# Two-layer hybrid encoder trunk: a new written order of the mixers' steps, with the output projection cut into half-steps

## The chip, the cores and the metric

The kernel runs on one core of a Trainium2 chip, in one launch. The metric is the device time of an execution in microseconds. The kernel before took 1021.98 us, the median of three runs (1021.69 to 1022.37).

Engine names are those of the profile: PE is the matrix engine (PEld its weight loads), DVE the vector engine, ACT the scalar engine, POOL the general one, and SP the queue that issues the weight transfers.

## The reference, cut to what matters

The input is 256 tokens of width 1024, in float32. Each of two layers does a half-step SwiGLU, a mixer, and a second half-step SwiGLU:

```python
for l in range(DEPTH):
    h_res = h_res + 0.5 * swiglu(rmsnorm(h_res, ffn1_norm[l]), ...)
    z = rmsnorm(h_res, mix_norm[l]) @ w_in[l]
    zq, zk, zv, zp, hq, hi, hff, hfb, hg = jnp.split(z, split_idx, axis=-1)
    y_att = dilated_attention(zq, zk, zv, q_norm[l], k_norm[l], biases)
    y_pool = pool_mixer(zp, pool_w[l], pool_scale[l])
    y_rec = hgrn2_bidirectional(hq, hi, hff, hfb, hg, ...)
    h_res = h_res + jnp.concatenate([y_att, y_pool, y_rec], axis=-1) @ w_out[l]
    h_res = h_res + 0.5 * swiglu(rmsnorm(h_res, ffn2_norm[l]), ...)
```

The attention has 8 heads of 64 with normalised queries and keys, a relative bias and a softmax. The pooling mixer has four window sizes. The recurrence (HGRN2) has 4 heads of 64 and runs in both directions. The concatenated 1024 columns go through one output projection of 1024 x 1024.

## The kernel before

Every large product is made of three float32r products: each operand is split into a high part (an ACT copy) and a low part (a DVE subtraction). The weights come as 512 KB "halves". For each half SP issues a transfer into one of four stage buffers, ACT makes `whi` (L149) and DVE `wlo` (L150). There are five buffers for split halves, and `ahead(i)` asks for the split of half i + 4 when half i is about to be used.

The text changed is in `mixer`. A step list `ORDER[l]`, one for each layer, writes out the order in which the mixer's steps are issued. PE and SP run exactly in the order of the program (`manual_schedule` for these two). DVE, ACT and POOL run fixed queues too, but their order is chosen when the kernel is built, by a planner: it takes what it believes to be ready, the earliest written first, and the steps `ga`, `gb`, `uv` and `up` are ranked ahead of their place. The planner also hands out the buffers of a pool. So a step's place in the list fixes PE's order, and influences that of DVE and ACT.

The steps, by their names in the list:

- `c:0` to `c:19` are the input projection's halves in the order hq, q, k, zh (pooling inputs and recurrence values), hg, v; q, k, zh and v take four quarter-steps each of 12 products of 512 columns, hq and hg two steps of 24 products of 256 columns. When the last one of a name is issued, its evacuation is issued: `qk_evac` (with squares and sums), `tok_evac` for zh and v, `hg_evac` (a chain of four ACT and three DVE operations).
- `ns`, `nq`, `nk` scale and turn the queries and keys into columns: four transposes, then a high part by ACT (L669, L675) and a low part by DVE (L670, L676).
- `mm:m`, `up:m`, `put:m` are the levels of the recurrence: 32 or 64 small products, the update of U and W by DVE (L523), and the storing of the result by DVE (L569) or ACT (L574, L579, L583). `join`, `rec`, `rn1`, `rn2` finish it: `rec` multiplies into `ops`, `rn1` squares and splits, `rn2` sums by two products (`hss`) and normalises.
- `sc:n` scores two heads: 12 products into two PSUM banks, then the softmax of each head. DVE adds the bias and takes the extreme (L701), ACT exponentiates (L704), DVE takes the reciprocal and scales (L706, L708).
- `tr:h` turns a head's probabilities (four transposes, L715) and ACT copies them out (L717). `pv:n` multiplies two heads by the values (L727); an odd one splits the result (L257, L258).
- `band`, `pool` make the pooling mixer: 16 products (L741) and a copy (L745), then 4 products (L751), two ACT and two DVE operations (L756, L757) on one bank.
- `o:name` is one quarter of the output projection's contraction, by `down`: two halves, `dh` 0 and 1, of 12 products of 512 columns each, into four tiles `wo`.

PSUM has eight banks, in two pools of four. Pool `pg` (tag "g") holds the projection's accumulators, the turns of q and k, scores, `pbs`, `hss`, `pps`, `pv` and, before, `ops`. Pool `py` (tag "y") holds the levels' results, the turned probabilities `tp`, and at the end the four `wo` tiles.

Of the kernel before, what the change touches and what calls it, by code (L numbers as in the profile page):

```python
# [8 lines left out]
F32 = mybir.dt.float32  # L9
# [7 lines left out]
P = 128  # L17
D = 1024
T = 256
# [24 lines left out]
OUT_NAMES = ("pool", "rec", "a0", "a1")  # L44
# [2 lines left out]

ORDER = (
    (
# [4 lines left out]
    ),  # L54
    (
# [4 lines left out]
    ),  # L60
)
LOOK = 4
# [8 lines left out]
class Trunk:  # L71
# [161 lines left out]
                self.mm3t(accs[tt], self.xh[:, k, s], self.xl[:, k, s], wh[:, kk, :], wl[:, kk, :],  # L233
                          start=(k == 0), stop=(k == KC - 1))

    def down(self, i, ys, ah, al, first, last, mid=None, post=None):

        for dh in range(2):
            self.ahead(i + dh)
            wh, wl = self.half(i + dh, 2)  # L240
            for tt in range(2):
                s = slice(tt * P, tt * P + P)
                for f in range(2):
                    self.mm3t(ys[2 * dh + tt], ah[:, f, s], al[:, f, s], wh[:, f, :], wl[:, f, :],
                              start=(first and f == 0), stop=(last and f == 1))
                if post is not None:
                    post(dh, tt)
            if dh == 0 and mid is not None:
                mid()
# [202 lines left out]
    def mixer(self, l):  # L452
        nc = self.nc
        mx, pg, py = self.mx, self.pg, self.py
        i0 = self.cur
        o0 = i0 + IN_HALVES
        V = {}
# [4 lines left out]
        def bank(name):  # L462
            return pg.tile([P, 2, T], F32, tag="g", name=name)
# [124 lines left out]
                nc.vector.tensor_copy(V["Ad"][p, :, p], V["A"][p])  # L588

        def rec_mm():  # L590
            ops = V["ops"] = bank("ops")
            vh = V["vh"]
            for hp in range(2):
                for e in range(2):
                    h = 2 * hp + e
                    for tb in range(2):
                        for n, sb in enumerate((tb, 1 - tb)):
                            A = V["Ad"][:, 2 * h + tb, :] if sb == tb else V["Ao"][:, 4 * sb + h, :]
                            nc.tensor.matmul(ops[e * 64:e * 64 + 64, hp, tb * P:tb * P + P],
                                             lhsT=vh[:, sb, h * 64:h * 64 + 64], rhs=A,  # L600
                                             start=(hp == 0 and tb == 0 and n == 0),
                                             stop=(hp == 1 and tb == 1 and n == 1), skip_group_check=True)
# [106 lines left out]

        def att_tr(h):  # L710
            pt = V["P", h]
            tp = py.tile([P, 2, T], F32, tag="y", name="tp")
            for kt in range(2):
                for qt in range(2):
                    nc.tensor.transpose(tp[:, kt, qt * P:qt * P + P], pt[:, qt, kt * P:kt * P + P], self.ident)  # L715
            pT = V["PT", h] = self.t2("PT")
            nc.scalar.activation(pT, tp, AF.Copy)  # L717
# [43 lines left out]
        ga, gb = bank("ga"), bank("gb")  # L761
# [23 lines left out]

        ys = []

        def out(nm):
            n = OUT_NAMES.index(nm)
            if n == 0:  # L790
                ys.extend(py.tile([P, 512], F32, tag="y", name="wo") for _ in range(4))
            src = V["yatt", int(nm[1])] if nm[0] == "a" else V["y" + nm]
            last = n == len(OUT_NAMES) - 1
            if last:
                self.new_xt()
            post = lambda dh, tt: self.add(ys[2 * dh + tt], 1.0, dh, tt, self.to_stage(3 * l + 2))
            self.down(o0 + 2 * n, ys, *src, first=n == 0, last=last, post=post if last else None)

        do = {
            "c": take, "ga": gates_a, "gb": gates_b, "uv": lev_init, "up": lev_up, "mm": lev_mm,  # L800
            "put": lev_put, "join": lev_join, "band": pool_band, "pool": pool_out, "ns": qk_scale, "nq": lambda j: qk_turn("q", j),
            "nk": lambda j: qk_turn("k", j), "sc": att_scores, "tr": att_tr, "pv": att_pv, "rec": rec_mm,
            "rn1": rec_squares, "rn2": rec_norm, "o": out,
        }
        for step in ORDER[l].split():
            nm, _, arg = step.partition(":")
# [163 lines left out]
```

## Time and profile before

| | before |
|---|---|
| median of three runs | 1021.98 us |
| the profiled execution, whole | 1022.51 us |
| its span, first to last instruction | 1020.7 us |
| PE busy | 1002.3 us (98%) |
| DVE busy | 606.7 us (59%) |
| ACT busy | 538.7 us (53%) |
| first mixer, first projection product to first product of the next SwiGLU | 199.95 to 327.46 us |
| second mixer, the same | 703.89 to 830.92 us |

The span is what the profiler saw of the program; the execution's own time has 1.8 us more around it. Times below are in us from the span's start. In a timeline row, a duration is from an instruction's start to the modelled end of its result, so that neighbouring matrix products overlap: their cost is the distance from start to start. "[0.60 <-DVE st L701]" at the end of a row says that the engine sat idle so long just before it, and what ended that. A row with "x4" merges four alike.

### The profile page before, as it was taken

What the parts mean: (1) busy time and instruction counts of PE and PEld (TensorE: products, weight loads), DVE (VectorE), ACT (ScalarE), POOL (GpSimd) and SP (SyncE); (2) the same over time, 40 slices, a digit from 0 to 9 for tenths busy, and PEclk for the clock granted to TensorE, in tenths of its full rate; (3) what the DMA queues carried; (4) which work ended last, traced back from release to release, by engine and by line L of the source; (5) the groups of instructions that cost most, each with busy time, mean ns of one, the idle gap of its engine ahead of it and who ended that gap; (6) DMA issues with size and microseconds to landing.
All of it is one profiled execution on the core that took longest, in us unless ns stands there. A gap on an engine that the chain in (4) does not pass through costs nothing.

```text
span 1020.7 us, 14464 instructions
## 1 busy us (share of the span) xinstructions
PE 1002.3 (98%) x5722; PEld 828.2 (81%) x5722; DVE 606.7 (59%) x811; ACT 538.7 (53%) x774; POOL 3.3 (0%) x8
## 2 busy tenths in 40 slices
PE   8999999999999999999999999999999999999998
PEld 7888788897877888888878888888877778888886
DVE  5555555689955655555565454556998465545453
ACT  7444444675765544444474444446857554444441
POOL 0000100000000000000000000000000000000000
PEclk9999999999999999999999999999999999999999
DMA  7675876544334556555655656554542345556551
GB/s 257 223 258 187 278 257 187 181 148 151 103 107 155 173 186 194 185 194 185 186 165 186 186 188 185 192 188 135 192 142 88 121 155 190 186 188 187 186 187 60
DMA packets 50276, 181.16 MB, mean 177 GB/s; under 512 B 5752, under 2 KB 6008, under 8 KB 49952
## 3 DMA queue, kind: packets, MB, share of 16 engines
q1 hardware_dynamic: 48528, 174.09, 53.4%
q0 software_dynamic: 720, 4.21, 1.2%
q10 hardware_dynamic: 960, 1.94, 0.5%
q8 instruction: 45, 0.74, 0.3%
q14 instruction: 23, 0.19, 0.1%
HBM read 179.15 MB, written 3.16 MB: 179 GB/s over the span
## 4 chain that ended last, share of the span: by engine, by line
PE 84%; DVE 8%; ACT 4%; issue 2%; DMA 1%; SPq 0%; DVEq 0%
PE gu L168 16%; PE gu L170 15%; PE gu L169 15%; PE ya L170 8%; PE ya L168 8%; PE ya L169 8%; DVE wlo L150 2%; ACT whi L149 2%; PE hp L352 2%; PE wo L168 1%; PE wo L170 1%; PE wo L169 1%; DVE P L701 1%; PE xps L294 1%; PE pv L727 1%
## 5 line engine op out<-in xcount | busy, mean ns | idle before, releaser
L150 DVE TENSOR_TENSOR wlo<-stage,whi 128x1024 fp32r<-128x1024 f32 (+1 forms) x329 | 401.4, 1222 | 350.1 <-ACT whi L149 349.3
L149 ACT ACTIVATE whi<-stage 128x1024 fp32r<-128x1024 f32 (+1 forms) x329 | 347.1, 1056 | 369.2 <-PE gu L170 200.1
L168 PE MATMUL gu<-whi,xh 128*128 128x512 f32 x704 | 275.4, 391 | 3.7 <-DVE xl L273 2.2
L170 PE MATMUL gu<-whi,xl 128*128 128x512 f32 x704 | 274.2, 390 | 0.0
L169 PE MATMUL gu<-wlo,xh 128*128 128x512 f32 x704 | 274.0, 389 | 0.0
L168 PEld LDWEIGHTS gu<-whi,xh 128*128 128x128 f32 x704 | 132.2, 188 | 33.1 <-DVE xl L273 2.9
L170 PEld LDWEIGHTS gu<-whi,xl 128*128 128x128 f32 x704 | 132.1, 188 | 28.3 <-DVE xl L273 0.9
L169 PEld LDWEIGHTS gu<-wlo,xh 128*128 128x128 f32 x704 | 132.2, 188 | 27.0
L168 PE MATMUL ya<-whi,hi 128*128 128x512 f32 x352 | 141.5, 402 | 0.0
L170 PE MATMUL ya<-whi,lo 128*128 128x512 f32 x352 | 137.7, 391 | 0.0
L169 PE MATMUL ya<-wlo,hi 128*128 128x512 f32 x352 | 137.3, 390 | 0.0
L170 PEld LDWEIGHTS ya<-whi,lo 128*128 128x128 f32 x352 | 66.0, 188 | 14.4
L169 PEld LDWEIGHTS ya<-wlo,hi 128*128 128x128 f32 x352 | 66.3, 188 | 12.6
L168 PEld LDWEIGHTS ya<-whi,hi 128*128 128x128 f32 x352 | 66.2, 188 | 12.3
L345 ACT ACTIVATE g<-gu,rc 128x256 f32<-128x256 f32 x88 | 41.4, 475 | 47.4 <-PE gu L170 47.4
L346 DVE SCALAR_TENSOR_TENSOR h<-gu,rc,g 128x256 f32<-128x256 f32 x88 | 42.0, 481 | 23.9 <-ACT g L345 23.9
L258 DVE TENSOR_TENSOR lo<-hp,hi 128x512 fp32r<-128x512 f32 x44 | 30.1, 684 | 2.8 <-ACT hi L257 2.8
L257 ACT ACTIVATE hi<-hp 128x512 fp32r<-128x512 f32 x44 | 25.5, 580 | 2.7 <-PE hp L352 2.7
L352 PEld LDWEIGHTS hp<-cst,h 128*128 128x128 f32 x176 | 21.8, 139 | 5.7
L352 PE MATMUL hp<-cst,h 128*128 128x128 f32 x176 | 26.3, 271 | 0.0
L272 ACT ACTIVATE xh<-xps,prm 128x256 fp32r<-128x256 f32 x48 | 20.5, 471 | 5.8 <-DVE xl L273 3.4
L273 DVE SCALAR_TENSOR_TENSOR xl<-xps,prm,xh 128x256 fp32r<-128x256 f32 x48 | 21.3, 478 | 2.4 <-ACT xh L272 2.2
(223 smaller groups left out, 997.5 us busy)
## 6 DMA issues: line engine op xcount, KB each, us to landing
stage<-w_all SPq DMA_DIRECT2D x327, 512.0 KB, 3.5
skew<-drow POOLq DMA_DIRECT2D x1, 2048.0 KB, 10.3
bias<-skew POOLq DMA_DIRECT2D x2, 1024.0 KB, 11.6
x<-x SPq DMA_DIRECT2D x4, 256.0 KB, 5.1
band<-band ACTq DMA_DIRECT2D x1, 1024.0 KB, 7.7
y_t<-x SPq DMA_DIRECT2D x4, 256.0 KB, 2.2
stage<-w_all SPq DMA_DIRECT2D x2, 256.0 KB, 5.5
mskf<-msk ACTq DMA_DIRECT2D x1, 320.0 KB, 5.7
```

The source lines that it names most:

```text
L149: nc.scalar.activation(hi[:, s], st[:, s], AF.Copy)
L150: nc.vector.tensor_tensor(lo[:, s], st[:, s], hi[:, s].bitcast(F32), op=ALU.subtract)
L168: nc.tensor.matmul(out, lhsT=ah, rhs=wh, start=start, stop=False, skip_group_check=True)
L169: nc.tensor.matmul(out, lhsT=ah, rhs=wl, start=False, stop=False, skip_group_check=True)
L170: nc.tensor.matmul(out, lhsT=al, rhs=wh, start=False, stop=stop, skip_group_check=True)
L257: self.nc.scalar.activation(hi, src, AF.Copy)
L258: self.nc.vector.tensor_tensor(lo, src, hi.bitcast(F32), op=ALU.subtract)
L272: nc.scalar.activation(self.xh[:, k, :], src, AF.Copy, scale=g)
L273: nc.vector.scalar_tensor_tensor(self.xl[:, k, :], src, g, self.xh[:, k, :].bitcast(F32), op0=ALU.mult, op1=ALU.subtract)
L345: silu = nc.scalar.activation(g2[:, tt, :], gu[tt][:, 0:256], AF.Silu, scale=r)
L346: nc.vector.scalar_tensor_tensor(h[:, tt, :], gu[tt][:, 256:512], r, g2[:, tt, :], op0=ALU.mult, op1=ALU.mult)
L352: nc.tensor.transpose(hp[:, f, tt * P:tt * P + P], h[:, tt, f * P:f * P + P], self.ident)
```

## The change

Three things change. (1) The two step lists are rewritten. The score steps move later: in the first layer from after c:12, c:13, c:14 and c:15 to after c:13, c:15, c:17 and into the output projection; in the second from after c:13 (two of them), c:14 and c:15 to after c:14, c:15, c:17 and into the output projection. `nq:0 nq:1` follow c:8 in both, and `band` moves from after c:16 to after c:14. In the first layer `nk:0 nk:1` stand together after c:12, the levels from 16 on come one step of c later, and `rec` moves from after c:16 to after c:17. The turns `tr` come mostly in pairs, and the last two, with `sc:3`, `pv:2` and `pv:3`, stand between half-steps of the output projection. (2) `o:name` becomes two steps `o:name/0` and `o:name/1`, by a new argument `dhs` of `down`. (3) `ops` moves from the pool `pg` to `py`, and a turn issued when the `wo` tiles exist takes its bank from `pg`. The instructions and their operands are otherwise the same, in number and shape.

```diff
 ORDER = (
     (
-        "c:0 ga c:1 gb c:2 uv c:3 c:4 mm:0 c:5 put:0 mm:1 up:2 ns:q c:6 put:1 c:7 mm:2 up:4 nq:0 c:8 put:2 nq:1 c:9 mm:4 up:8 ns:k put:4 "
-        "c:10 c:11 mm:8 up:16 put:8 nk:0 c:12 nk:1 mm:16 up:32 put:16 sc:0 c:13 mm:32 up:64 put:32 sc:1 "
-        "c:14 mm:64 up:128 put:64 sc:2 tr:0 c:15 mm:128 put:128 join tr:1 sc:3 c:16 tr:2 band rec rn1 c:17 rn2 tr:3 tr:4 pool c:18 tr:5 tr:6 "
-        "c:19 tr:7 o:pool pv:0 pv:1 o:rec pv:2 pv:3 o:a0 o:a1 "
+        "c:0 ga c:1 gb c:2 uv c:3 c:4 mm:0 c:5 put:0 mm:1 up:2 ns:q c:6 put:1 c:7 mm:2 up:4 c:8 put:2 nq:0 nq:1 c:9 mm:4 up:8 ns:k put:4 "
+        "c:10 c:11 mm:8 up:16 put:8 c:12 nk:0 nk:1 c:13 sc:0 mm:16 up:32 put:16 c:14 mm:32 up:64 put:32 band "
+        "c:15 sc:1 tr:0 tr:1 mm:64 up:128 put:64 c:16 mm:128 put:128 join c:17 rec rn1 sc:2 tr:2 tr:3 c:18 rn2 pool tr:4 tr:5 "
+        "c:19 o:pool/0 pv:0 pv:1 sc:3 o:pool/1 o:rec/0 tr:6 tr:7 o:rec/1 pv:2 pv:3 o:a0/0 o:a0/1 o:a1/0 o:a1/1 "
     ),
     (
-        "c:0 ga c:1 gb c:2 uv c:3 c:4 c:5 mm:0 ns:q put:0 c:6 mm:1 up:2 put:1 c:7 nq:0 c:8 mm:2 up:4 nq:1 put:2 c:9 ns:k mm:4 up:8 put:4 "
-        "c:10 c:11 mm:8 up:16 put:8 c:12 nk:0 nk:1 c:13 sc:0 mm:16 up:32 put:16 sc:1 c:14 mm:32 up:64 put:32 "
-        "sc:2 tr:0 c:15 mm:64 up:128 put:64 tr:1 sc:3 c:16 tr:2 band mm:128 put:128 join c:17 tr:3 tr:4 rec rn1 pool c:18 rn2 tr:5 tr:6 "
-        "c:19 tr:7 o:pool pv:0 pv:1 o:rec pv:2 pv:3 o:a0 o:a1 "
+        "c:0 ga c:1 gb c:2 uv c:3 c:4 c:5 mm:0 ns:q put:0 c:6 mm:1 up:2 put:1 c:7 c:8 nq:0 nq:1 mm:2 up:4 put:2 c:9 ns:k mm:4 up:8 put:4 "
+        "c:10 c:11 mm:8 up:16 put:8 c:12 nk:0 nk:1 c:13 mm:16 up:32 put:16 c:14 mm:32 up:64 put:32 sc:0 band "
+        "c:15 mm:64 up:128 put:64 sc:1 c:16 mm:128 put:128 join tr:0 tr:1 c:17 rec rn1 sc:2 tr:2 c:18 rn2 pool tr:3 tr:4 "
+        "c:19 tr:5 o:pool/0 pv:0 pv:1 sc:3 o:pool/1 o:rec/0 tr:6 tr:7 o:rec/1 pv:2 pv:3 o:a0/0 o:a0/1 o:a1/0 o:a1/1 "
     ),
 )
...
-    def down(self, i, ys, ah, al, first, last, mid=None, post=None):
-
-        for dh in range(2):
+    def down(self, i, ys, ah, al, first, last, mid=None, post=None, dhs=(0, 1)):
+
+        for dh in dhs:
...
         def rec_mm():
-            ops = V["ops"] = bank("ops")
+            ops = V["ops"] = py.tile([P, 2, T], F32, tag="y", name="ops")
...
         def att_tr(h):
             pt = V["P", h]
-            tp = py.tile([P, 2, T], F32, tag="y", name="tp")
+            tp = bank("tp") if ys else py.tile([P, 2, T], F32, tag="y", name="tp")
...
-        def out(nm):
-            n = OUT_NAMES.index(nm)
-            if n == 0:
+        def out(part):
+            nm, dh = part.split("/")
+            n, dh = OUT_NAMES.index(nm), int(dh)
+            if n == 0 and dh == 0:
                 ys.extend(py.tile([P, 512], F32, tag="y", name="wo") for _ in range(4))
             src = V["yatt", int(nm[1])] if nm[0] == "a" else V["y" + nm]
             last = n == len(OUT_NAMES) - 1
-            if last:
+            if last and dh == 0:
                 self.new_xt()
             post = lambda dh, tt: self.add(ys[2 * dh + tt], 1.0, dh, tt, self.to_stage(3 * l + 2))
-            self.down(o0 + 2 * n, ys, *src, first=n == 0, last=last, post=post if last else None)
+            self.down(o0 + 2 * n, ys, *src, first=n == 0, last=last, post=post if last else None, dhs=(dh,))
```

## Rows read from the trace of the kernel before

**Rows 1.** The profile's page, part 1: busy time, share of the span, instructions.

```profile
PE 1002.3 (98%) x5722; PEld 828.2 (81%) x5722; DVE 606.7 (59%) x811; ACT 538.7 (53%) x774; POOL 3.3 (0%) x8
```

**Rows 2.** Waits of PE, first mixer (199 to 330): total us, times, longest.

```profile
PE sc L692 <- DVE Lk L670: 1.2, 1, 1.2
...
PE tp L666 <- DVE zk L657: 0.6, 2, 0.3
PE pbs L741 <- DVE st L701: 0.6, 1, 0.6
PE tp L666 <- DVE zq L657: 0.6, 2, 0.4
PE pps L751 <- ACT rrs L613: 0.4, 1, 0.4
```

**Rows 3.** Waits of PE, second mixer (705 to 842).

```profile
PE pbs L741 <- DVE st L701: 1.5, 1, 1.5
PE tp L666 <- DVE zq L657: 0.8, 1, 0.8
...
PE sc L692 <- DVE st L701: 0.5, 1, 0.5
PE sc L692 <- DVE Lk L670: 0.5, 1, 0.5
```

**Rows 4.** Busy us by window: length, then PE, PEld, DVE, ACT, POOL.

```profile
240.00:270.00 30.00, 28.22 (x392) 23.01 (x392) 27.82 (x56) 16.73 (x35) 0.00 (x0) 1.00 0.39 117
...
300.00:330.00 30.00, 28.97 (x147) 22.04 (x146) 16.73 (x20) 14.64 (x25) 0.00 (x0) 1.00 0.45 142
```

**Rows 5.** Timeline of PE: start, duration, instruction; second mixer's first and third turn.

```profile
773.56 0.66 PE L715 MATMUL tp<-cst,P 128*128 128x128 f32 x4
773.98 0.36 PE L161 MATMUL hg<-xh,whi 128*128 128x256 f32 x1
...
782.45 0.60 PE L715 MATMUL tp<-cst,P 128*128 128x128 f32 x4
784.54 0.44 PE L741 MATMUL pbs<-band,uh 128*64 128x256 f32 x2 [1.50 <-DVE st L701]
```

**Rows 6.** Timeline of PE: a two-half output step; a level step.

```profile
298.60 0.48 PE L168 MATMUL wo<-whi,yh 128*128 128x512 f32 x1
...
304.25 1.95 PE L727 MATMUL pv<-PT,va 128*64 128x256 f32 x16
...
269.86 0.27 PE L552 MATMUL lev<-U,W 64*64 64x64 f32 x1
...
270.93 0.39 PE L692 MATMUL sc<-Hk,Hq 64*128 64x256 f32 x2
```

**Rows 7.** Timelines of PE and ACT: second mixer's second turn, two copies.

```profile
778.10 0.66 PE L715 MATMUL tp<-cst,P 128*128 128x128 f32 x4
...
776.83 0.60 ACT L717 ACTIVATE PT<-tp 128x512 f32<-128x512 f32 x1
...
783.34 0.60 ACT L717 ACTIVATE PT<-tp 128x512 f32<-128x512 f32 x1
```

**Rows 8.** Timelines of PE and DVE: last scores and last scaling, first mixer.

```profile
261.48 0.39 PE L692 MATMUL sc<-Hk,Lq 64*128 64x256 f32 x2
...
265.92 0.62 DVE L708 TENSOR_SCALAR P<-P,st 128x256 f32<-128x256 f32 x2
...
277.65 0.28 PE L692 MATMUL sc<-Hk,Lq 64*128 64x256 f32 x2
...
285.58 0.62 DVE L708 TENSOR_SCALAR P<-P,st 128x256 f32<-128x256 f32 x2
```

**Rows 9.** Timelines of PE, ACT and DVE: pooling output, first mixer.

```profile
290.91 1.13 PE L751 MATMUL pps<-pm,prm 128*128 128x256 f32 x4 [0.39 <-ACT rrs L613]
...
295.92 0.48 ACT L756 ACTIVATE yh<-pps,prm 128x256 fp32r<-128x256 f32 x1
...
297.22 0.48 DVE L757 SCALAR_TENSOR_TENSOR yl<-pps,prm,yh 128x256 fp32r<-128x256 f32 x1
```

## The prediction, written before the result was known

> **What bounds the kernel now.** I read the page first, then the waits of PE in each mixer, then the busy time by windows, then the timelines around each wait.
>
> The page says that PE is busy 98% of the span [rows 1]. So only 18.4 us of 1020.7 are there to be won on PE, as long as its work stays the same, and this change leaves every product and its shape as it was. DVE and ACT, at 59% and 53%, can only cost time where they make PE wait.
>
> The waits of PE say where. In the first mixer five groups belong to steps that move: 1.2 us before the first scores, 0.6 before the turns of k, 0.6 before the pooling band, 0.6 before the turns of q, 0.4 before the pooling output; in sum 3.4 us in 7 waits [rows 2]. In the second mixer they are 1.5 (band), 0.8 (turns of q), 0.5 and 0.5 (scores): 3.3 us in 4 waits [rows 3]. Together 6.7 us in 11 waits.
>
> A wait costs more than its idle time, because the stream of products starts anew. A turn's four transposes take 0.42 us from start to start when the next step runs on; where the band behind them waits 1.50 us, the distance is 2.09 us [rows 5]. That is 0.17 more than 0.42 + 1.50. With 0.19 for each of 11 waits (I round up for the wait that stretched the scores' other products) the waits cost 6.7 + 2.1 = 8.8 us. This is the most that the change can win.
>
> The windows say why PE waits. From 240 to 270 us DVE is busy 27.82 of 30 us; from 300 to 330, where the output projection runs, 16.73 of 30 [rows 4]. The softmaxes stand in the full stretch, and the change takes them out of it, the last one into the empty one.
>
> **The change, part by part.**
>
> *Instructions.* None is added or removed. The halves keep their order, so each `ahead` issues the same split for the same half in the same sequence: SP's list of transfers is unchanged, POOL has no part in the mixers, and no moved step issues a transfer. An output step of two halves (24 products) takes 5.65 us [rows 6], so a half-step takes 2.83, and I use the same for a quarter-step of 12 products. Cutting one in two adds only a switch between streams; the old list paid as many at other places. Zero, from −0.3 to +0.5 us.
>
> *The turns of q and k.* They now follow one more quarter-step (`nq:0` after c:8, `nk:0` after c:12), so DVE's scaling has 2.83 us more. The longest wait of these was 0.8 [rows 3]: all three groups go, 0.6 + 0.6 + 0.8 = 2.0 us. If DVE came later by the whole 2.83 they would stay; it has the same work ahead of it there.
>
> *First scores.* In the first layer they stood one level step after the turn of k and waited 1.2 us for the turn's bank [rows 2]. Now c:13 lies between, which is the order that the second layer had before, and that one waited 0.5 [rows 3]. I count 0.5 as left (bounds 0 and 1.2). In the second layer c:14 is put between as well, and its 0.5 goes. The other 0.5 there, scores waiting for the bank of the scores before, goes because half a mixer now lies between two scores.
>
> *Band and pooling output.* The band waited for a score bank. Behind the new order no scores stand just before it in the first layer, and in the second they stand right before it but need two of four banks, with one taken by hg: the fourth is free. Both waits (0.6, 1.5) go. The output's 0.4 was a wait for a bank of `pg`; with `ops` in `py` one more is free, and it goes.
>
> *New: turns before the last level, first layer.* `tr:0 tr:1 mm:64` now hold all four banks of `py`, and `mm:128` needs two. Its banks come free by ACT's copies. From the end of tr:1 to `mm:128` PE has one level step, 270.93 − 269.86 = 1.07 us [rows 6], and c:16, 2.83: 3.9 us. How long after a turn is its copy done? In the second mixer, 776.83 + 0.60 − 774.22 (773.56 + 0.66) = 3.2 us in one case [rows 5, 7] and 783.34 + 0.60 − 778.76 = 5.2 us in another [rows 7]; the second copy of a pair is up to 0.6 later. So the wait lies between 0 and 1.9; I take 1.0, the middle, since the exponentials of sc:1 and the four ACT operations of hg stand in ACT's queue ahead of those copies. Behind PE's wait only PE's own steps are queued.
>
> *New: the third softmax.* sc:2 stands 4.9 us before the turn of its first head: two turns 0.84, c:18 2.83, and `hss` and `pool`, two 512-column and four 256-column products, about 1.2 (an estimate at 0.235 us for 512 columns, from the 24 in 5.65). From the last scores to the last scaling DVE and ACT took 266.54 − 261.87 = 4.7 us at sc:0 and 286.20 − 277.93 = 8.3 us at sc:3 [rows 8]. The latter ran among hg's chain, which is now issued two quarter-steps before sc:2. I take 0.4 in each mixer (bounds 0 and 3.4).
>
> *New: the fourth softmax in the output projection.* From sc:3 to tr:6 lie two half-steps, 5.65 us. Against 4.7 that is enough, against 8.3 it is 2.65 too short. DVE is little more than half busy there [rows 4]: I take 0.2 in each mixer. The splits of the weights are hidden by the four halves that they run ahead; pv:2 follows its turns by a half-step, and the split of its result has two half-steps before `a1` uses it.
>
> *New: the pooling output close to its use.* Before, it was ready 297.70 − 292.04 = 5.7 us after its products, with other work put between its four operations; alone they need 4 x 0.48 = 1.9 us [rows 9]. Now `o:pool/0` starts 0.84 + 2.83 = 3.7 us after them, and reads the last piece 1.2 us into it: 0 to 0.8 late; I take 0.3 in each mixer.
>
> *Sum.* Won: 8.8. New waits: 0.5 + 1.0 + 2 x (0.4 + 0.2 + 0.3) = 3.3, and about four restarts at 0.2, 0.8. Net 4.7 us. The profiled execution took 1022.51 us (span 1020.7, 1.8 around it), 0.5 above the median of 1021.98; the net comes off either: 1022.5 − 4.7 = 1017.8 for that execution, 1021.98 − 4.7 = **1017.3 us** as a median.
>
> *A rule that speaks against this.* In the kernel before no turn of probabilities waited: none is among the waits of the mixers [rows 2, 3]. The Trainium skill, "Perfetto Trace Analysis", Optimization Strategy, says that bubbles that return on the engine that should be full can mean too little PSUM for the next tile. By that, moving `ops` to the pool of the turns and pairing them is the wrong direction. The first scores' wait agrees with it, in the other pool. By the rows the sum stays as above; by the rule the first rival holds.
>
> **The rivals.**
>
> *The waits move to the banks of `py`.* Each place where a level, `ops` or a `wo` tile follows a pair of turns waits for the pair's copies, as worked out for `mm:128`, at the upper end of 1.9 us. There are two such places in each mixer (before the last level or `ops`, and before the third and fourth `wo`). 4 x 1.9 = 7.6 of the 8.8 are taken back: 1020.8 us, between 1020 and 1022. For it: four banks for turns, levels and `ops`. Against it: after most pairs a quarter-step or more lies in between.
>
> *All is covered.* DVE, eased where it was full, meets every new date: 1021.98 − 8.8 = 1013.2 us. For it: nearly all of the waits end on DVE. Against it: ACT's queue is fixed and 8.3 us did occur.
>
> *Slower: the softmax's latency.* If sc:2 and sc:3 take L = 8.3 us to the last scaling in their new places too, because weight splits are put in front of them, PE waits 8.3 − 4.9 at the turns of sc:2 and 8.3 − 5.65 at tr:6, in each mixer: 12.1 us in place of the 1.2 that I count for the two. With the other new waits (0.5 + 1.0 + 0.6) that makes 1021.98 − 8.8 + 14.2 = 1027.4 us. It decides from L = 7.0: 2 x (2L − 10.55) = 8.8 − 2.1. For it: the scores measured last in the old kernel. Against it: those lay among hg's chain.
>
> **How the numbers follow.** Forecast 0.57, banks 0.20, covered 0.15, latency 0.08. A measurement of this kernel can tell about 0.2% (2.0 us) from no change, so faster means below 1019.9 and slower above 1024.0. Of the forecast nearly all (0.56) and all of "covered" lie below 1019.9: 0.71. The banks' case is mostly within: 0.18 with a remainder of the forecast. Slower: latency 0.08 and 0.03 for a poor order of DVE's and ACT's queues elsewhere: 0.11. The forecast's own range is 1015 to 1019.5; the range that holds 8 in 10 runs from 1014.0, into "covered", to 1022.0, the end of the banks' case.
>
> **What would show it.** Right: waits of PE before the turns of q and k, the band and the pooling output gone; a wait of about 1 us before `mm:128` in the first mixer, ended by ACT's copy of a turn; small ones at the turns of heads 4 and 6; DVE in the middle of the mixers below 9 tenths; each mixer some 2 to 3 us shorter, everything outside equal. Wrong: turns or `ops` or `wo` that wait at every pair (banks), turns that wait for DVE's scaling by more than 1.5 us (latency), or any lengthening of the SwiGLU stages, which nothing here explains.

## The result, and the profile after

The changed kernel took 1016.79 us (median of four runs, 1016.74 to 1017.16) against 1022.17 (1021.69 to 1022.48) for the kernel before on the same chip: a ratio of 0.9949, 95% interval 0.9936 to 0.9962. The forecast was 1017.3 us, a gain of 4.7; 5.4 was measured. The profiled execution took 1017.16 us, its span 1015.4.

First the page's busy times and its row of PE's granted clock over the span, where each digit is a fortieth of the span and 9 means nine tenths of full speed or more.

```profile
PE 1002.1 (99%) x5722; PEld 827.2 (81%) x5722; DVE 607.6 (60%) x811; ACT 539.2 (53%) x774; POOL 3.3 (0%) x8
...
PEclk9999999999999999999999999999999999999999
```

PE's work is what it was [rows 1]; the span lost 5.3 us of PE's idle time and restarts. The stages, cut at PE's first product of each, show where:

| us | up to first mixer | first mixer | SwiGLUs between | second mixer | rest |
|---|---|---|---|---|---|
| before | 199.95 | 127.52 | 376.43 | 127.03 | 189.81 |
| after | 199.71 | 124.86 | 376.47 | 124.53 | 189.79 |

The mixers are 2.66 and 2.50 us shorter and nothing else moved. (The stretch up to the first mixer has the same instructions in all kernels here and lay between 198.96 and 199.95 us; a median carries up to 1 us of that, so parts are compared below by the mixers' lengths.)

The waits of PE over the whole span (total us, times, longest):

```profile
PE gu L168 <- DVE xl L273: 2.2, 3, 0.7
PE xps L294 <- DVE x L371: 1.6, 5, 0.3
PE ga L161 <- DVE xl L273: 1.5, 2, 0.7
PE gu L168 <- ACT xh L272: 1.2, 2, 1.0
PE wo L168 <- ACT yh L756: 1.1, 4, 0.6
PE idle L818 <- DVE ones L125: 1.1, 1, 1.1
PE lev L544 <- DVE W L523: 0.2, 1, 0.2
```

All 11 waits of [rows 2, 3] are gone. Two are new: the first products of the output projection wait for the pooling output `yh`, and one level waits 0.2 us for U and W. The other rows belong to the normalisations around the SwiGLUs and to the kernel's start, and were there before.

Busy time by windows, the columns as in [rows 4]:

```profile
240.00:270.00 30.00, 30.00 (x413) 25.08 (x412) 27.87 (x52) 17.97 (x34) 0.00 (x0) 1.00 0.46 146
300.00:330.00 30.00, 28.92 (x146) 22.84 (x145) 17.91 (x34) 17.26 (x35) 0.00 (x0) 1.00 0.47 142
```

PE is now busy in all 30 us of the first window. DVE is as full there as it was, 27.87 against 27.82: PE stopped waiting for an engine that got no emptier.

PE's timeline at the places where new waits were expected, the last row from the second mixer:

```profile
270.87 0.28 PE L692 MATMUL sc<-Hk,Lq 64*128 64x256 f32 x2
271.08 1.09 PE L715 MATMUL tp<-cst,P 128*128 128x128 f32 x8
...
276.14 0.37 PE L556 MATMUL lev<-U,W 64*128 64x128 f32 x1
...
283.39 0.28 PE L692 MATMUL sc<-Hk,Lq 64*128 64x256 f32 x2
...
292.03 0.39 PE L170 MATMUL v<-whi,xl 128*128 128x512 f32 x1
293.04 0.51 PE L168 MATMUL wo<-whi,yh 128*128 128x512 f32 x1 [0.62 <-ACT yh L756]
...
294.47 0.50 PE L168 MATMUL wo<-whi,yh 128*128 128x512 f32 x1 [0.17 <-ACT yh L756]
...
296.80 1.95 PE L727 MATMUL pv<-PT,va 128*64 128x256 f32 x16
...
299.37 0.28 PE L692 MATMUL sc<-Hk,Lq 64*128 64x256 f32 x2
...
794.04 0.50 PE L168 MATMUL wo<-whi,yh 128*128 128x512 f32 x1 [0.15 <-ACT yh L756]
```

ACT's timeline of the same places:

```profile
275.06 1.05 ACT L717 ACTIVATE PT<-tp 128x512 f32<-128x512 f32 x2
...
289.06 0.67 ACT L613 ACTIVATE rrs<-hss,cols 128x512 f32<-128x512 f32 x1
289.76 0.63 ACT L614 ACTIVATE rrs<-rrs 128x512 f32<-128x512 f32 x1
291.10 0.69 ACT L682 ACTIVATE va<-v,rc 128x512 f32<-128x512 f32 x1 [0.70 <-PE v L170]
292.00 0.63 ACT L257 ACTIVATE hi<-rrs 128x512 fp32r<-128x512 f32 x1 [0.21 <-DVE rrs L626]
292.53 0.46 ACT L756 ACTIVATE yh<-pps,prm 128x256 fp32r<-128x256 f32 x1
...
293.93 0.48 ACT L756 ACTIVATE yh<-pps,prm 128x256 fp32r<-128x256 f32 x1
```

And DVE's, the last scalings of the second, the third and the fourth softmax:

```profile
278.07 0.62 DVE L708 TENSOR_SCALAR P<-P,st 128x256 f32<-128x256 f32 x2
...
287.48 0.62 DVE L708 TENSOR_SCALAR P<-P,st 128x256 f32<-128x256 f32 x2
...
302.81 0.62 DVE L708 TENSOR_SCALAR P<-P,st 128x256 f32<-128x256 f32 x2
```

Four things are to be read here. `mm:128`, for which a wait of 1.0 us was forecast, starts at 276.14; ACT's second copy of the turns ended at 275.06 + 1.05 = 276.11, so it was just in time, and no wait shows. From sc:2 to its last scaling it took 288.10 − 283.67 = 4.4 us, from sc:3 303.43 − 299.65 = 3.8 us, and no turn waits for them. (From sc:1, which now runs beside hg's chain, it took 278.69 − 271.15 = 7.5 us; its turns come later.) The products of `pps` were ready at 288.79, but ACT's queue has `yh` behind both steps of `rrs`, a copy of v for which ACT itself sits idle 0.70, and the high part of `rrs`: it comes 3.7 us later. PE pays for that: from c:19's start to the output step's it is 3.62 us where 2.85 is usual, and the half-step takes 296.80 − 293.04 = 3.76 where 2.83 was counted, 1.7 us in all; 1.3 in the second mixer.

### The profile page after: what moved, and what is told of

Its sections match the earlier page's. It is cut to its first block, busy times and chain, and to the rows that moved or that the text cites. A ratio compares the mean times of both kernels' runs of the same rounds, so it can differ in the third digit from the quotient of the medians.

```text
span 1015.4 us, 14477 instructions
## 1 busy us (share of the span) xinstructions
PE 1002.1 (99%) x5722; PEld 827.2 (81%) x5722; DVE 607.6 (60%) x811; ACT 539.2 (53%) x774; POOL 3.3 (0%) x8
## 4 chain that ended last, share of the span: by engine, by line
PE 93%; ACT 3%; DVE 3%; DMA 1%; issue 0%; SPq 0%; ACTq 0%
PE gu L168 16%; PE gu L170 16%; PE gu L169 16%; PE ya L170 8%; PE ya L168 8%; PE ya L169 8%; PE hp L352 2%; PE lev L544 1%; PE wo L168 1%; PE wo L170 1%; PE wo L169 1%; ACT whi L149 1%; DVE wlo L150 1%; PE zh L168 1%; PE xps L294 1%; PE pv L727 1%
```

## The experiments

The theory at the start was the prediction's: PE waited because DVE was full in the middle of the mixers, and the new order takes the softmaxes out. The rival: DVE's load does not matter, but how far in PE's order a step stands behind the work it needs, given fixed queues. Each run below names its ratio to the kernel before, run beside it.

### The turns of q and k alone

```diff
 # both mixers: the turns of q (second mixer: "c:7 c:8 nq:0 nq:1 mm:2 up:4 put:2")
-"nq:0 c:8 put:2 nq:1 c:9"
+"c:8 put:2 nq:0 nq:1 c:9"
 # first mixer: the turns of k
-"nk:0 c:12 nk:1 mm:16"
+"c:12 nk:0 nk:1 mm:16"
```

> The kernel before with one edit: the turns of q and k stand where the change puts them (nq:0 nq:1 after c:8, nk:0 nk:1 after c:12); scores, band, pool, rec and the output projection stay. Theory (a wait that is given a quarter-step more goes): the five waits before these turns go, 0.6 + 0.6 + 0.8 us idle and about 0.2 for each restart, 2.9 us in all; the first scores of the first layer, right behind the turn of k, may take up to 1.2 of it back. 1020 to 1021 us against 1022.2. Rival (DVE is full there, so the wait only moves on to the next step that needs DVE): 1022, no change.

Measured: 1020.0 us (1019.59 to 1021.19), 0.9984 [0.9975, 0.9992]. The second mixer became 1.20 us shorter, the first 0.13 us longer. PE's waits of the first mixer from 240 us on, and single windows there:

```profile
PE sc L692 <- DVE Lk L670: 1.3, 2, 1.1
...
PE lev L544 <- DVE W L523: 0.4, 1, 0.4
```

```profile
259.00:260.00 1.00, 1.00 (x12) 0.86 (x13) 1.00 (x3) 0.00 (x0) 0.00 (x0) 1.00 0.71 250
...
261.00:262.00 1.00, 1.00 (x4) 0.81 (x3) 1.00 (x6) 0.60 (x2) 0.00 (x0) 0.50 0.01 4
...
264.00:265.00 1.00, 1.00 (x43) 0.64 (x44) 0.80 (x4) 1.00 (x5) 0.00 (x0) 1.00 0.00 0
```

The waits before the turns went, as the theory had it, and in the first mixer new ones came behind them, as the rival had it. On top of it the granted clock fell after those waits, for some 3 us (the column after POOL: 1.00, then 0.50, then 1.00 again). The last section comes back to that.

### The tail alone

```diff
 # first mixer (the second likewise), with o: cut in two by `dhs`
-"tr:1 sc:3 c:16 ... tr:5 tr:6 c:19 tr:7 o:pool pv:0 pv:1 o:rec pv:2"
+"tr:1 c:16 ... tr:5 c:19 o:pool/0 pv:0 pv:1 sc:3 o:pool/1 o:rec/0 tr:6 tr:7 o:rec/1 pv:2"
```

> The kernel before with the tail alone: sc:3, tr:6 and tr:7 between the half-steps of the output projection as in the change; everything up to sc:2 stays. Theory: the scores no longer stand before the pooling band, so its waits of 0.6 and 1.5 us go with their restarts, and the softmax in the emptier tail costs nothing: 1019.5 to 1020 us. Rival one (the band waits for DVE whatever stands before it): 1022. Rival two (latency of the softmax of up to 8.3 us in the tail): 2 x 2.7 us more on the other side, 1024 to 1025.

Measured: 1019.46 us (1018.92 to 1019.8), 0.9975 [0.9965, 0.9985]; the mixers lost 0.91 and 1.82 us. The waits of `band` are gone, those before the turns and scores stand as before (one of them 0.4 in place of 0.5 us). As the theory had it.

### DVE made emptier, order as before

```diff
             def put(m): # levels 1 to 16
-                for d in range(2):
-                    n = 2 * LEVELS.index(m) + d
-                    nc.vector.copy_predicated(V["A"], self.msk[...], v(ps[d]))
+                pass
```

> The kernel before, in its old order, with the ten predicated copies of DVE (L569, 0.74 us each, 7.4 us in each mixer) left out in each layer; the levels 1 to 16 of the recurrence are then not stored. Nothing on PE moves. Theory (PE's waits in the mixers come from DVE being full between 240 and 270 and between 750 and 780 us): most of the 8.8 us of waits go, 1014 to 1017 us. Rival (they come from the order, a step standing too close behind what it needs, whatever DVE's load): at most 2 us, 1020 to 1022.

Measured: 1022.2 us (1021.96 to 1022.82), 1.0002 [0.9993, 1.0011]. The kernel leaves out the storing of those levels. The window 240 to 270, then PE's waits of the first mixer (two lines of code fewer stand above these), then ACT and DVE before the first scores:

```profile
240.00:270.00 30.00, 28.25 (x416) 23.17 (x414) 22.90 (x51) 17.22 (x37) 0.00 (x0) 1.00 0.38 125
```

```profile
PE pbs L739 <- DVE st L699: 1.5, 1, 1.5
PE sc L690 <- DVE Lk L668: 1.2, 1, 1.2
...
PE tp L664 <- DVE zk L655: 0.6, 2, 0.3
...
PE tp L664 <- DVE zq L655: 0.4, 1, 0.4
```

```profile
257.01 1.06 ACT L149 ACTIVATE whi<-stage 128x1024 fp32r<-128x1024 f32 x1 [2.17 <-PE zh L170]
...
258.10 1.23 DVE L150 TENSOR_TENSOR wlo<-stage,whi 128x1024 fp32r<-128x1024 f32 x1 [1.55 <-ACT whi L149]
259.24 0.68 DVE L668 TENSOR_TENSOR Lk<-tp,Hk 128x512 fp32r<-128x512 f32 x1
```

DVE's 27.82 us became 22.90, and PE's waits came to 7.1 us in 9 waits in the two mixers, against 6.7 in 11. Those before the first scores (1.2) and the turns of k of the first mixer are as long as they were. Others changed place: one before the turns of q and two before scores went, the band's grew from 0.6 to 1.5 and from 1.5 to 1.8 us, and a level of the second mixer waits 0.4. The last rows show why less work on DVE did not help the first scores: `Lk`, which ends their wait, stands in DVE's queue behind `wlo`, and DVE sits idle 1.55 us there until ACT, which was itself waiting for PE, has made `whi`. The reason that the prediction gave falls; the rival holds. Two limits: the queues of DVE and ACT were planned anew for this kernel, and the copies left out stood 11 us and more ahead of the band, so of the band's waits it says little.

### DVE's and ACT's order changed, work and PE's order as before

```diff
-                ev[nm](acc[nm])
+                with self.tc.high_priority(offset=FIRST) if nm in ("q", "k") else nullcontext():
+                    ev[nm](acc[nm])
...
-            with self.tc.high_priority(offset=FIRST) if nm in ("ga", "gb", "uv", "up") else nullcontext():
+            with self.tc.high_priority(offset=FIRST) if nm in ("ga", "gb", "uv", "up", "ns") else nullcontext():
```

> The kernel before with the evacuation of q and k (squares, sums, root) and their scaling ranked ahead of their place in the written order, as the steps ga, gb, uv and up are. PE's order and the amount of work on DVE and ACT stay the same; only the order of those two queues changes. Since leaving out a quarter of DVE's work there changed nothing, the theory is now: PE's waits come from the order of the fixed queues, a needed operation standing behind others that wait themselves. Then the waits before the turns of q and k (0.6 + 0.6 + 0.8 us idle, with restarts some 2.8) shrink by at least half: 1019.5 to 1020.8 us against 1022.2. Rival (the chain from the last product of q to its scaling is as long as that whatever its rank): 1022.

Measured: 1021.15 us (1020.75 to 1023.88), 0.9995 [0.9987, 1.0004]; the mixers lost 0.90 and 0.09 us. PE's waits, first mixer:

```profile
PE sc L692 <- DVE Lk L670: 1.4, 1, 1.4
...
PE lev L544 <- DVE W L523: 0.6, 1, 0.6
```

No turn of q or k waits any more, so the order of the queues did decide that. But the level behind waits 0.6 us for U and W (0.9 in the second mixer), and the first mixer's scores 1.4 in place of 1.2. PE reaches the next step that needs DVE earlier, and stops there. So the waits that were to shrink did, but the 1019.5 to 1020.8 us expected from that did not come: 0.75 us were won by the medians, and the interval of the ratio includes 1.

### `ops` in the other pool alone

```diff
-            ops = V["ops"] = bank("ops")
+            ops = V["ops"] = py.tile([P, 2, T], F32, tag="y", name="ops")
```

> The kernel before with ops in the pool py and nothing else. Theory (the bank that it frees in pg removes the wait of the pooling output, 0.4 us and a restart of 0.2, in the first mixer alone): 1021.5 against 1022.1. Rival (in py it takes a bank from the turns, which then wait for its release by DVE): 1023 to 1025.

Measured: 1021.29 us (1020.94 to 1021.62), 0.9992 [0.9983, 1.0]. The pooling output's wait of 0.4 us in the first mixer is gone and that mixer is 0.72 us shorter, the second the same; no wait for a bank of `py` came in its place.

### Turns and tail together

The edits of the first two runs in one kernel.

> The kernel before with the moves of the turns of q and k (alone 1020.0 us) and of the tail (alone 1019.5 us) together; sc:0 to sc:2, band, rec, pool and ops stay. If the two parts are independent, 2.1 + 2.7 us add up: 1017.3. Theory: the rest of the change (scores, band and pool moved in the middle, ops in py) then won only 0.5 us net, because it takes away about 3 us of waits at the first scores, the second scores and the pooling output and adds about 3 us at the first output half-step, which this kernel does not have. Rival (the parts overlap): 1018.5 or more.

Measured: 1018.87 us (1017.17 to 1019.32), 0.9961 [0.9948, 0.9975]. The second mixer lost 2.98 us, the sum of the parts (1.20 + 1.82). The first lost only 0.21, with the same waits before the level and the scores (0.42, 1.10 and 0.22 us) and the same fall of the clock as in the turns alone. The median lies where the rival had it. But two of the five runs have a mean granted clock of 1.000, at 1017.17 and 1017.76 us, 4.4 and 5.0 us below the kernel before: there the parts nearly add up to the 4.8 expected, and the rest of the change is worth 0.4 to 1.0 us, plus what it gains by keeping the clock up.

### The pooling output's step earlier

```diff
 # changed kernel; first mixer, and behind "join tr:0 tr:1" in the second
-"join c:17 rec rn1 sc:2 tr:2 tr:3 c:18 rn2 pool tr:4 tr:5"
+"join pool c:17 rec rn1 sc:2 tr:2 tr:3 c:18 rn2 tr:4 tr:5"
```

> The changed kernel with the step pool two steps of c earlier, before c:17 in both mixers; nothing else is edited. Theory (the first output half-step is late because the pooling output is evacuated late, behind what stands in ACT's queue): about 1.7 us goes in the first mixer and 0.9 to 1.3 in the second, 1013.8 to 1014.5 us against 1016.8. Rival (those operations, put earlier, hold up the copies of the levels' results or the turns that rec waits for, in the stretch where ACT is busiest): 1016 to 1018.

Measured: 1014.7 us (1014.2 to 1014.72), 0.9924 [0.9912, 0.9937]. The mixers are 1.72 and 0.62 us shorter than in the changed kernel; no product waits for the pooling output any more. The median is 0.2 us above the range expected: the second mixer gave 0.62 in place of 0.9 to 1.3. One product of its output projection now waits 0.3 us for a copy of a turn by ACT, which it does not read, that is for a bank of `py`.

### The pooling output in room of its own, PE's order as changed

```diff
-            yh, yl = V["ypool"] = self.t2("yh", F32R), self.t2("yl", F32R)
+            yp = tl("k", [P, 4, T], F32R)
+            yh, yl = V["ypool"] = yp[:, 0:2, :], yp[:, 2:4, :]
```

> The changed kernel with one edit: the two parts of the pooling output (yh, yl) get a tile of their own (the room of k, free by then) in place of two of the sixteen shared ones. PE's order is the same. Theory (in the changed kernel the first output half-step waits because the sixteen shared tiles are all taken when the pooling output is evacuated, so the planner had to place yh late in ACT's queue): the wait of 0.6 + 0.2 us with its restart goes in the first mixer and 0.35 in the second, and with the slow first half-step 1.7 + 1.3 us in all: 1013.8 to 1014.5 us against 1016.8. Rival (the queue's order there follows from what ACT and DVE have to do, not from room): 1016.8.

Measured: 1014.6 us (1014.16 to 1014.85), 0.9928 [0.9914, 0.9941]; the mixers are 1.54 and 0.75 us shorter than in the changed kernel, where 1.7 and 1.3 were expected. ACT's timeline (the high part is now named `k`, and one line of code more stands above it):

```profile
288.39 0.68 ACT L613 ACTIVATE rrs<-hss,cols 128x512 f32<-128x512 f32 x1
288.96 0.47 ACT L757 ACTIVATE k<-pps,prm 128x256 fp32r<-128x256 f32 x1
289.32 0.63 ACT L614 ACTIVATE rrs<-rrs 128x512 f32<-128x512 f32 x1
```

The high part stands right behind the first step of `rrs`, three places further ahead, and no product of the output projection waits. So its late place had come from room: `yh` and `yl` were taken from 16 shared tiles, and with a tile of their own and nothing else changed they come in time. That all sixteen were taken there is concluded from this; the trace does not show tiles. The planner wrote the shortage down as a late place in ACT's queue. The Trainium skill ("Perfetto Trace Analysis", Optimization Strategy) says that gaps that return on the engine that should be full can mean too little room for the next tile. The trace agrees, but at one remove: PE's 0.62 us is ended by ACT, and only ACT's order shows the lack.

### The last turns one half-step earlier

```diff
-"sc:3 o:pool/1 o:rec/0 tr:6 tr:7 o:rec/1"
+"sc:3 o:pool/1 tr:6 tr:7 o:rec/0 o:rec/1"
```

> The changed kernel with tr:6 tr:7 one half-step earlier in the output projection, 2.83 us behind the last scores in place of 5.65. In the changed kernel the last scaling of sc:3 ends 3.8 us after the last scores, that of its first head 2.8. Theory (the softmax in the tail takes about 3.8 us, so one half-step is too little by about 1 us and two are enough): a wait of 0.5 to 1.1 us with restart before tr:7 in each mixer, 1018 to 1019 us against 1016.8. Rival (the latency in the tail is set by what the planner puts in front, and shrinks when the turns are wanted earlier): 1016.8. Second rival (8 us latency, as before the change among the recurrence's chain): 1025.

Measured: 1018.32 us (1017.94 to 1018.58), 0.9961 [0.9948, 0.9973]; each mixer 0.59 us longer than in the changed kernel. PE:

```profile
302.59 0.60 PE L715 MATMUL tp<-cst,P 128*128 128x128 f32 x4
303.44 0.72 PE L715 MATMUL tp<-cst,P 128*128 128x128 f32 x4 [0.25 <-DVE P L708]
```

One half-step is too short for the softmax and two are enough, which agrees with the 3.8 us read above.

### The last scores moved back out of the output projection

```diff
 # changed kernel; first mixer (in the second: "pool sc:3 tr:3 tr:4 c:19 tr:5 tr:6 tr:7 o:pool/0")
-"rn2 pool tr:4 tr:5 c:19 o:pool/0 pv:0 pv:1 sc:3 o:pool/1 o:rec/0 tr:6 tr:7 o:rec/1"
+"rn2 pool sc:3 tr:4 tr:5 c:19 tr:6 tr:7 o:pool/0 pv:0 pv:1 o:pool/1 o:rec/0 o:rec/1"
```

> The changed kernel with the last scores and turns moved back out of the output projection: sc:3 stands behind `pool`, tr:6 and tr:7 behind c:19 and ahead of the first wo product; scores in the middle, turns of q and k and `ops` stay as changed. From sc:3 to tr:6 lie two turns and c:19 in the first mixer, 0.84 + 2.83 = 3.7 us, and three turns and c:19 in the second, 4.1 us. Theory (a softmax takes a latency that PE's steps must span; it was 3.8 us between the halves of the output projection and 4.4 behind c:18, where DVE and ACT have more to do): PE waits 0.3 to 1.5 us for the scaling at tr:6 in each mixer, as it did when one half-step lay between. Against that the scores' step between the pooling products and the output projection gives the pooling output about 1 us more, which takes most of the waits of 0.6 us before wo away. Together 1017.5 us, between 1016 and 1020: the place inside the output projection is worth 0 to 3 us. Rival (the spacing in the middle of the mixer does all of it, and the place between the halves nothing): no wait at tr:6, the wait before wo smaller, 1015 to 1016.2.

Measured: 1031.33 us (1029.94 to 1031.49), 1.0087 [1.0073, 1.0101]. Both expectations missed, by 11 us and more: the mixers are 6.2 and 7.3 us longer than in the changed kernel. PE's timeline in the first mixer, DVE's, and the windows:

```profile
287.10 1.02 PE L751 MATMUL pps<-pm,prm 128*128 128x256 f32 x4
289.11 0.38 PE L692 MATMUL sc<-Hk,Hq 64*128 64x256 f32 x1 [0.99 <-ACT rrs L613]
294.15 0.58 PE L692 MATMUL sc<-Hk,Hq 64*128 64x256 f32 x1 [4.66 <-DVE yl L757]
```

```profile
293.61 0.48 DVE L757 SCALAR_TENSOR_TENSOR yl<-pps,prm,yh 128x256 fp32r<-128x256 f32 x1 [0.54 <-ACT yh L756]
```

```profile
288.00:291.00 3.00, 0.51 (x2) 0.18 (x1) 2.43 (x3) 1.69 (x3) 0.00 (x0) 1.00 0.11 19
291.00:294.00 3.00, 0.00 (x0) 0.00 (x0) 1.70 (x4) 1.47 (x3) 0.00 (x0) 0.51 0.43 156
```

The scores do not read `rrs` or `yl`. What these free are banks: of the four of `pg`, v's two accumulators hold two until c:19 ends, `hss` holds one until `rrs` has read it (289.06), and `pps` one until the second `yl` has read it (294.09). The scores need two and start as these come free. No turn waits for a softmax; the latency that both expectations argued about played no part. Here the rule on room of the Trainium skill ("Perfetto Trace Analysis", Optimization Strategy), which the prediction weighed, does hold, in `pg`: the same gap stands in both mixers, 4.7 us each. So the place between the halves of the output projection is worth more than its latency: there `hss` and `pps` are done with and their banks free. How much more is not separated: `yh` is late here as in the changed kernel (ACT makes it at 291.86, 3.7 us after `pps` is ready at 288.12, behind the high part of `rrs`), and that is what holds the last bank. No run has the scores at this place and the pooling output in room of its own.

### Everything that was found, together

The changed kernel with the pooling output in its own room; in the second mixer `mm:2 up:4` ahead of the turns of q, `pool` ahead of `rn2`, and `tr:5` ahead of c:19.

```diff
 # second mixer
-"c:8 nq:0 nq:1 mm:2 up:4 put:2" ... "c:18 rn2 pool tr:3 tr:4 c:19 tr:5 o:pool/0"
+"c:8 mm:2 up:4 nq:0 nq:1 put:2" ... "c:18 pool rn2 tr:3 tr:4 tr:5 c:19 o:pool/0"
```

> The changed kernel with the pooling output in a tile of its own (alone 1014.6 us) and three moves in the second mixer: mm:2 up:4 ahead of the turns of q, pool ahead of rn2, tr:5 ahead of c:19. The step after c:9 there waits 0.2 us and costs 0.35 more than its like, the first output half-step 0.45: theory, both go: 1013.6 to 1014.0 us. Rival (each wait removed there is replaced by the next one): 1014.6.

Measured: 1013.74 us (1013.5 to 1014.07), 0.9920 [0.9906, 0.9933], the mixers 123.30 and 123.12 us. The only waits of PE left in the mixers are those for their normalised input.

The same with `pool` ahead of c:17 in both mixers:

> As the kernel with the pooling output's own tile and the three moves in the second mixer, but with pool before c:17 in both mixers. If the room and the early step cure the same wait, no gain over the former: 1013.6 to 1014.3 us. If what is left at the first output half-step of the second mixer is the lateness of the pooling output, 0.4 us less.

Measured: 1013.68 us (1013.42 to 1014.28), 0.9920 [0.9907, 0.9934], the mixers 123.30 and 123.12: no more is to be had from that.

## Why the prediction was right, and where its reason was not

*The gain of 8.8 us.* Right in the main. All 11 waits went. What they were worth shows best in the kernel with everything that was found, whose steps wait nowhere in the mixers: 127.52 − 123.30 + 127.03 − 123.12 = 8.1 us. Of this 6.7 were idle time, which leaves 1.4 for 11 restarts, 0.13 us each where 0.19 was counted (if the other moves in that kernel cost nothing). That a wait costs more than its idle time was sound, the size a little high. The case "all is covered", at 1013.2 us, is nearly what that kernel reached, 1013.74.

*Why PE waited.* Wrong. "DVE is busy 27.82 of 30 us, therefore PE waits" was read from a window, and a full engine beside a wait is not yet its cause: with 4.9 us less on DVE the time stayed the same, and in the changed kernel DVE is as full and PE doesn't wait. The sign that went with it, DVE below 9 tenths in the middle of the mixers, did not come (27.87 of 30). What decides is where a step stands in PE's order behind the last operation that it needs, in queues whose order is fixed. And what the step lacked was mostly a bank: by the prediction's own readings only the turns' waits, 2.0 of the 6.7 us, were for data. The other 4.7 were for banks of `pg` that DVE or ACT had yet to release. PE's timeline before shows it at the first scores: a first product goes, and the next, which reads the same tiles and needs the second bank, waits.

```profile
259.35 0.38 PE L692 MATMUL sc<-Hk,Hq 64*128 64x256 f32 x1
260.89 0.38 PE L692 MATMUL sc<-Hk,Hq 64*128 64x256 f32 x1 [1.17 <-DVE Lk L670]
```

The run with other ranks shows why single cures gain little: the next step that needs DVE takes the wait over. The turns alone gained about 2.4 us where the clock held, the tail 2.7, and only in the changed kernel, with the levels and scores spread too, did the waits at scores and levels in the first mixer go.

*`mm:128` behind ACT's copies, 1.0.* No wait shows. The distance of 3.9 us was right (276.14 − 272.17 = 4.0), the copies' latency (276.11 − 272.17 = 3.9) lay between the two cases that were read. That they met to 0.03 us is luck. The first rival, banks of `py`, falls with it, and with the run of `ops` alone; its mechanism was seen once, at 0.3 us, with the pooling output earlier.

*First scores in the first layer, 0.5, and the third and fourth softmax, 0.4 and 0.2 in each mixer.* All 0. The softmaxes took 4.4 and 3.8 us, below the lower of the two cases, 4.7 [rows 8]. That hg's chain no longer runs beside them is the likely reason: sc:1, which has it beside it now, took 7.5 us in the same trace. No run moved the chain alone. The slower rival needed 7.0 us at sc:2 and sc:3. (The 1.2 us for `hss` and `pool` does not follow from 0.235 us for 512 columns, which gives 0.9; 288.63 − 287.30 = 1.3 was measured, so the distance was right.) At the fourth the turns start at 305.16, 1.7 us after the last scaling; the run with the turns one half-step, 2.83 us, earlier shows that this is all there is to spare.

*The pooling output, 0.3 in each mixer.* This is the term that was mis-sized: 1.7 and 1.3 us in the timelines (1.54 and 0.75 came back when it got its own room), where 0.8 was the upper bound. It was worked out from four operations of 0.48 us one behind the other, and missed what stands ahead of them on ACT, which shared room had put there.

*The sum.* By the mixers 5.2 us were won where 4.7 were forecast. Two errors partly cancel: the old waits were worth 8.1 and not 8.8, the new ones with their restarts cost about 3.0 and not 4.1, one place taking nearly all. (The 4.1 also counted four restarts for eight new waits.) So the agreement of the totals is in part luck and says little for the single terms: of five kinds of new waits four were not there, and the fifth was four to six times its size.

*Banks.* The prediction put the danger into `py`. It was in `pg`, just beside the path taken: the order with the scores moved back, which looks harmless by latencies, loses 14.5 us against the changed kernel, with the late pooling output as part of the cause.

## What to carry to other kernels

Where one engine bounds and the others have slack, look for each wait's distance in the bound engine's own order to the operation that it waits for, and move steps until that distance spans the latency, counted to the release of a bank as well as to the data; emptying the engine that ends the wait may do nothing. Move all the steps of a stretch together, since a cured wait passes to the next dependent step. For each moved step count the tiles and banks that are taken at its new place, as carefully as its time: in an order chosen at build, lack of tiles showed here only as an operation oddly late in a queue, and lack of banks as a product released by an operation whose result it does not read.

## What the hardware did that was not expected

The granted clock fell from 1.00 to 0.50 of 2.4 GHz, the 1.2 GHz level, after PE had stood still more than once within a few us. In the turns alone that was 0.42 and, in two parts, 1.32 us, with one level of small products between them, and it seems to have happened in some executions only: five of its eleven runs had a mean granted clock of 0.997 or 0.998 and took 1020.46 to 1021.19 us; the six at 0.999 or 1.000 took 1019.59 to 1020.0. In the run with other ranks (waits of 0.59 and 1.35 us) two of eleven runs had 0.996 and 0.998, at 1023.88 and 1022.67 us, the others 1020.75 to 1021.46; those two were not profiled, so where their clock fell is not seen. By the medians of the two groups such a fall costs some 1.3 us in the turns alone and more here, nearly as much as the waits ahead of it. In the kernel before, waits of 0.61 and 1.17 us with more full work between them left the clock at 1.00. With the scores moved back PE stood 5.65 us but for one product, and all five runs had 0.993; from 294.15 to the turns at 295.73 the scores' products took 1.6 us, where they take 0.91 in the changed kernel. The Trainium skill, "TensorE: Matmul & The Clock Gate", "What's actually happening", says of the clock's rise at a kernel's start that its point differs between runs of one kernel; here it is the fall that differed, in five of eleven runs against the other six. No run here varied the length of a wait by itself, so how long a pause is still safe stays open.
